# Out-projection weights of a Hymba-style block: ready-made high and low parts of the weight sums

## The chip, the cores and the metric

One core of one Trainium2 chip runs the whole kernel. The metric is the device time of one execution in microseconds (us); the median of three runs is quoted for the kernel before.

## The reference

One decoder layer on x of 2048 tokens x 1024 channels (D_MODEL), float32 throughout:

```python
h = rmsnorm(x, norm_pre_mix)
z = h @ w_in                    # columns: gMLP u, v; FoX q, k, v, gate; memory q
out_a = gmlp_spatial_gating(g_u, g_v, gmlp_w_s, gmlp_b_s, gmlp_v_norm)
out_b = forgetting_attention(f_q, f_k, f_v, log_sigmoid(f_gate + b_forget))
out_c = memory_cross_attention(m_q, rmsnorm(mem), w_mem_kv)
y = concatenate([out_a, out_b, out_c]) @ w_out
x = x + rmsnorm(y, norm_post_mix)
f = square(relu(rmsnorm(x, norm_pre_ffn) @ w_ff1)) @ w_ff2
x = x + rmsnorm(f, norm_post_ffn)
```

gMLP has 6 groups of 64 channels and works in chunks of 128 tokens, forgetting attention has 6 heads of 64 with a causal mask, memory attention 4 heads over 256 memory rows. w_out is 1024 x 1024, w_ff1 1024 x 4096.

## The kernel before

**Arithmetic.** A float32 factor is held as two parts of a rounded format: hi is the rounded value (ACT copies it), lo the rest (`src - hi`, on DVE unless told otherwise; `split`, L194 to 197). A product is three matmuls, hi·hi, hi·lo and lo·hi (`mm3`, L203 to 205). Large products use a seven-product scheme over 2 x 2 blocks: instead of eight block products there are seven, taken in the order 1, 7, 2, 6, 4, 5, 3, of sums of blocks. Products 1, 2 and 3 take a block of the weights as it is; 7, 5, 6 and 4 take a sum.

**Stages.** For each half s = 0, 1 of the tokens a rows stage (norm, transposes, value columns) is followed by a columns stage (`columns_stage`) with four jobs n = 0 to 3 that make the queries, keys and memory queries. Then come attention and gating in one stage, whose instructions on PE, DVE, ACT and POOL stand in an order that a planner (`plan`) works out from costs and due times written beside each `op`, the out-projection (`out_pair(j)`, a pair of token tiles at a time), and the feed-forward part.

**The weight sums of the out-projection.** w_out is read as 2 x 2 blocks of 512 x 512, in four slices kk = 0 to 3 of 128 rows. `out_sums(kk, sc)` runs behind job n = kk of the columns stage of s = 0. It loads both row slices into `wor{kk}` (1 MB, from a pool of two tiles that the jobs' own weights `wrc` share), makes four sums on DVE (L518 to 521; the tiles `wos` share four buffers with the jobs' weight sums `sc`) and stores each as float32 (L523) in the DRAM tensors `ws_d`.

**How the sums are used.** `out_weights` (L951) is part of the plan. For m = 1, 7, 2, 6 (EARLY) and each kk it loads a 128 x 512 slice (SP, L959), rounds it (ACT, L966, `wo0`) and makes the low part (DVE, L969, `wo1`), in the attention stage's last stretch. `late_weights` (L1275) does the same for m = 4, 5, 3 (LATE) through `fill` at the out-projection's start: loads of L264, splits of L195 and L197. As its float32 pieces need room, `low` tiles of one m serve as the raw tile of another.

**Around it.** The out-projection reads the context of the attention as `cr{j}` (SP, L1290; two tiles in turn), sums it on POOL (L1294 to 1297, `cs`), splits it (`cx`), multiplies and adds up `y`; y4's second half is a sum on POOL (`added(nc.gpsimd, ...)`, L1329). In the attention, `s` are scores (PE, L826 and 827), `k` and `q` the keys and queries loaded by SP (L189, L699), `cb` the forgetting bias rows (L802), `v` the values, `hr` the rows for the gating product (L986), `pt`, `ph`, `pl` the softmax's numbers with their high and low parts (DVE, L753, makes `pl`), `pv` the product with the values (PE, L767), `gl` a low part in the gating (POOL, L1167). SP issues DMA transfers in the order of its rows; a row that waits holds those behind it.

Of the kernel before, what the change touches and what calls it, by code (L numbers as in the profile page):

```python
# [16 lines left out]
P = 128  # L17
# [34 lines left out]
class Plan:  # L52
# [11 lines left out]
    def op(self, engine, time, fn, after, at, takes=(), frees=(), late=0.0):  # L64
        o = Op(engine, time, fn, after, at, takes, frees, late)
        self.ops.append(o)
        return o
# [62 lines left out]
def kernel(  # L130
# [35 lines left out]
    def dram(name, shape, dt=F32):  # L166
        return dp.tile(shape, dt, name=name, tag=name)
# [8 lines left out]
    x1_d = dram("x1_d", [NT, P, D], F32)  # L176
    bq_d = [dram(f"bq{s}", [4, P, 4, KT // 2, P]) for s in range(NSB)]
    b_d = [{m: dram(f"b{s}_{m}", [P, 4, KT // 2, P]) for m in range(1, 8)} for s in range(NSB)]
    ws_d = {m: dram(f"ws_{m}", [KT // 2, P, 512]) for m in (7, 5, 6, 4)}
    vm_d = dram("vm_d", [P, 2, NMH, 2 * HD])  # L180
    km_d = [dram(f"km{w}", [2, P, NM]) for w in range(2)]
    hid_d = [
# [326 lines left out]

    def out_sums(kk, sc):  # L510

        raw = rp.tile([P, 2, D], F32, name=f"wor{kk}", tag="raw")
        for half in range(2):
            r0 = (half * KH + kk) * P
            nc.sync.dma_start(raw[:, half], w_out[r0 : r0 + P, :])
        b11, b12, b21, b22 = [raw[:, a, b * 512 : (b + 1) * 512] for a in range(2) for b in range(2)]
        sm = {m: sc.tile([P, 512], F32, name=f"wos{kk}_{m}", tag="s") for m in (7, 5, 6, 4)}
        nc.vector.tensor_tensor(out=sm[7], in0=b22, in1=b12, op=ALU.subtract)  # L518
        nc.vector.tensor_tensor(out=sm[5], in0=b12, in1=b11, op=ALU.subtract)
        nc.vector.tensor_tensor(out=sm[6], in0=b22, in1=sm[5], op=ALU.subtract)  # L520
        nc.vector.tensor_tensor(out=sm[4], in0=b21, in1=sm[6], op=ALU.subtract)
        for m, t in sm.items():
            nc.sync.dma_start(ws_d[m][kk], t)  # L523


    def memory_keys(w1p, cp_):
# [60 lines left out]
    def columns_stage(s, h):  # L587
        with ExitStack() as st:
# [7 lines left out]
            for n, (ca, cb, *to) in enumerate(jobs):  # L596
                nm = f"c{s}_{n}"
                if n == 0:
                    raws = [xp.tile([P, D], F32, name=f"wr{i}{nm}", tag="x") for i in range(2)]
                    raws = [t.rearrange("p (k c) -> p k c", k=KH) for t in raws]  # L600
                else:
                    raw = rp.tile([P, KT, 2 * P], F32, name=f"wr{nm}", tag="raw")
                    raws = [raw[:, :KH], raw[:, KH:]]
                w = column_weights(
                    raws, sc, w1p, nm, (w_in[:, ca : ca + P], w_in[:, cb : cb + P]), True,
                    nc.gpsimd if n else nc.vector,
                )

                def emit(f, tn, c, own, nm=nm, to=to):
                    scale, dst, p = to[3 * f : 3 * f + 3]  # L610
                    hi = cp_.tile([P, 512], F32R, name=f"oh{f}{tn}_{nm}", tag="oh")
                    lo = cp_.tile([P, 512], F32R, name=f"ol{f}{tn}_{nm}", tag="ol")
                    split(hi, lo, c, scale=scale)
                    t0 = s * SB + tn * 512
                    store(dst[0][p][:, t0 : t0 + 512], hi)
                    store(dst[1][p][:, t0 : t0 + 512], lo)

                pend = columns(nm, w, h, kp, cp_, (ps_x, "x"), (ps_y, "y"), emit, pend)
                if s == 0:
                    out_sums(n, sc)  # L620
                elif n == 0:
                    forget_sums()
                elif n == 1:
                    memory_keys(w1p, cp_)
                elif n == 2:
                    gating_weights(row_weights("wua"), range(4))
# [11 lines left out]

    def out_block(m, kk):

        if m in ws_d:
            return ws_d[m][kk]
        r0, c0 = {1: (0, 0), 2: (KH, 0), 3: (KH, 512)}[m]
        return w_out[(r0 + kk) * P : (r0 + kk + 1) * P, c0 : c0 + 512]

    def flat(w, kk):
        return w[:, kk].rearrange("p k t -> p (k t)")
# [2 lines left out]
    with ExitStack() as st:  # L650
# [36 lines left out]
        def chain(name, new):  # L687

            new.after.append(order.get(name))
            order[name] = new  # L690
            return new
# [258 lines left out]

        def out_weights(near, after, at):  # L951

            for n in range(len(EARLY) * KH):
                m, kk = EARLY[n // KH], n % KH
                t = {}

                def wload(n=n, m=m, kk=kk, t=t):
# [14 lines left out]

                o = op("SP", 0.73, wload, [near], at, takes=["p", "wor"], late=3.0)
                o = chain("wh", op("ACT", 0.478, whigh, [o, after], at))
                op("DVE", 0.602, wlow, [o], at, frees=["p", "wor"])

        held = []
# [289 lines left out]
    with ExitStack() as st:  # L1267
# [5 lines left out]
        gpre = bcast_row(io, norm_pre_ffn[0], D, "gain_pre2")  # L1273

        def late_weights():  # L1275
            raws = dict(zip(LATE, [low[LATE[0]], low[LATE[2]], extra]))
            lows = dict(zip(LATE, [low[LATE[1]], low[LATE[0]], low[LATE[2]]]))
            wo.update(
                fill("wo", LATE, raws, lows, high, lambda m: [
                    (lambda t, k=k: flat(t, k), out_block(m, k), None, ()) for k in range(KH)  # L1280
                ])
            )
            low.update(lows)

        def out_pair(j):

# [369 lines left out]
```

## Time and profile before

| | before |
|---|---|
| median of 3 runs | 2270.11 us (2264.58, 2270.87, 2270.11) |
| the profiled execution's own time | 2261.8 us |
| its span in the profile | 2260.0 us |
| mean granted TensorE clock | 0.988 |
| PE busy | 2166.3 us (96%) |

The span runs from the first to the last instruction of the profiled execution. PE is the matmul engine, PEld its weight loads, DVE the vector engine, ACT the scalar engine, POOL GpSimd, SP the engine whose queue issues most DMA transfers (SPq in the rows). A busy share is an average over stages, so the windows of single stages say more than the totals.

### The profile page before, as it was taken

Reading aid. Unit: us, or ns where it says so; the run is one execution under the profiler, and the core shown is the slowest. Engines: PE = TensorE matmul, PEld = TensorE weight load, DVE = VectorE, ACT = ScalarE, POOL = GpSimd, SP = SyncE. Lnnn points to the kernel's source line nnn. Section 1 sums busy time; section 2 is a strip of 40 time slices with the busy share of each in tenths; the row PEclk is TensorE's granted clock in tenths of the full one; section 3 lists DMA queues with packets and bytes.
Section 4 is the critical chain, followed back from the end, with each engine's and each line's share of the span. In section 5 each row is a group of like instructions: output and inputs, shape, how many; then the busy total and the mean of one; then the engine's idle time right before and its main releaser. Section 6 shows DMA issues by size and latency. Waiting matters only on the chain.

```text
span 2260.0 us, 33156 instructions
## 1 busy us (share of the span) xinstructions
PE 2166.3 (96%) x10468; PEld 1820.0 (81%) x10468; DVE 1646.4 (73%) x3137; ACT 1354.3 (60%) x2929; POOL 1030.5 (46%) x1073
## 2 busy tenths in 40 slices
PE   7999989999999989998999999999999999999997
PEld 7787778888888867876888878888788888888885
DVE  8778667777867789895333366555579998999888
ACT  6455567878877766665555576666654443444333
POOL 5444432443535255544333335446465445534524
PEclk9999999999999999999999999999999999999999
DMA  7775685365363265786333365565132212221277
GB/s 248 261 252 174 226 224 132 88 169 137 95 157 95 79 216 202 246 307 205 112 109 110 112 205 195 192 231 199 56 130 86 91 48 95 92 94 57 94 253 296
DMA packets 236843, 359.98 MB, mean 159 GB/s; under 512 B 24806, under 2 KB 141420, under 8 KB 235644
## 3 DMA queue, kind: packets, MB, share of 16 engines
q1 hardware_dynamic: 224380, 316.92, 44.4%
q0 software_dynamic: 12288, 40.95, 4.9%
q8 instruction: 83, 1.36, 0.3%
q14 instruction: 92, 0.75, 0.1%
HBM read 232.88 MB, written 124.91 MB: 158 GB/s over the span
## 4 chain that ended last, share of the span: by engine, by line
PE 74%; DVE 8%; DMA 7%; issue 4%; ACT 4%; POOL 2%; SPq 1%; DVEq 0%; POOLq 0%; ACTq 0%
PE gx L205 5%; PE gx L204 5%; PE gx L203 5%; PE fxf L204 5%; PE fxf L203 5%; PE fxf L205 5%; PE pt L745 3%; PE gy L205 2%; PE gy L204 2%; PE gy L203 2%; PE fyf L203 2%; PE fyf L204 2%; PE fyf L205 2%; PE pv L767 2%; PE pv L766 2%
## 5 line engine op out<-in xcount | busy, mean ns | idle before, releaser
L205 PE MATMUL fxf<-h,w_f 128*128 128x512 f32 x512 | 201.1, 393 | 4.5 <-DVE w_f L197 4.5
L203 PE MATMUL gx<-w,hc 128*128 128x512 f32 x512 | 199.0, 391 | 5.9 <-DVE ya L1539 5.9
L204 PE MATMUL fxf<-h,w_f 128*128 128x512 f32 x512 | 200.6, 392 | 2.3 <-DVE h L197 2.3
L195 ACT ACTIVATE hc<-hs 128x256 fp32r<-128x256 f32 x224 | 93.6, 418 | 181.3 <-PE gx L205 105.7
L203 PE MATMUL fxf<-h,w_f 128*128 128x512 f32 x512 | 200.8, 392 | 1.0 <-ACT w_f L195 0.5
L204 PE MATMUL gx<-w,hc 128*128 128x512 f32 x512 | 199.7, 390 | 0.0
L205 PE MATMUL gx<-w,hc 128*128 128x512 f32 x512 | 195.9, 390 | 0.0
L197 DVE TENSOR_TENSOR w_f<-sf,w_f 128x512 fp32r<-128x512 f32 x128 | 95.4, 745 | 134.1 <-ACT w_f L195 132.3
L1539 DVE TENSOR_TENSOR ya<-gx,ya 128x512 f32<-128x512 f32 x232 | 156.5, 683 | 40.8 <-PE gx L205 40.6
L753 DVE TENSOR_TENSOR pl<-pt,ph 128x512 fp32r<-128x512 f32 x240 | 140.8, 605 | 45.3 <-ACT ph L749 43.6
L866 ACT ACTIVATE p<-p,nm 128x512 f32<-128x512 f32 (+2 forms) x240 | 156.9, 657 | 22.5 <-DVE nm L856 22.2
L749 ACT CAST ph<-pt 128x512 fp32r<-128x512 f32 x240 | 120.4, 523 | 59.5 <-PE pt L745 51.7
L197 DVE TENSOR_TENSOR w_f<-wrf,w_f 128x512 fp32r<-128x512 f32 x96 | 80.8, 841 | 88.4 <-ACT w_f L195 88.4
L195 ACT ACTIVATE w_f<-sf 128x512 fp32r<-128x512 f32 x128 | 80.8, 632 | 102.2 <-PE fxf L204 57.2
L837 DVE CUSTOM_DVE_ANT_0 p<-s,cb 128x512 f32<-128x512 f32 (+2 forms) x216 | 124.7, 593 | 16.8 <-PE pt L745 9.4
L197 DVE TENSOR_TENSOR hc<-hs,hc 128x256 fp32r<-128x256 f32 x224 | 128.1, 574 | 7.3 <-ACT hc L195 7.2
L195 ACT ACTIVATE hc<-hr 128x256 fp32r<-128x256 f32 x168 | 68.4, 417 | 103.2 <-PE gx L205 66.7
L745 PE MATMUL pt<-ident,p 128*128 128x128 f32 x816 | 124.0, 277 | 2.7 <-ACT p L866 2.7
L816 POOL TENSOR_TENSOR cm<-cb,cmask 128x128 f32<-128x128 f32 x96 | 44.8, 467 | 171.3 <-DVE mx L837 140.9
L1379 POOL TENSOR_TENSOR hs<-hr 128x256 f32<-128x256 f32 x56 | 51.7, 923 | 152.0 <-DMA hr<-hid 79.9
L745 PEld LDWEIGHTS pt<-ident,p 128*128 128x128 f32 x816 | 102.3, 143 | 22.6 <-ACT p L866 2.9
L203 PEld LDWEIGHTS gx<-w,hc 128*128 128x128 f32 x512 | 96.3, 188 | 27.4 <-DVE ya L1539 7.6
(389 smaller groups left out, 7105.8 us busy)
## 6 DMA issues: line engine op xcount, KB each, us to landing
wrf<-in_w_ff_dram SPq DMA_DIRECT2D x64, 512.0 KB, 4.8
hid<-c_f SPq DMA_DIRECT2D x128, 256.0 KB, 2.5
hr<-hid SPq DMA_DIRECT2D x56, 512.0 KB, 4.3
w2r<-in_w_ff_dram SPq DMA_DIRECT2D x16, 1024.0 KB, 6.7
b<-ty POOLq DMA_DIRECT2D x56, 256.0 KB, 3.7
hs<-lh SPq DMA_DIRECT2D x56, 256.0 KB, 2.7
hc<-hs SPq DMA_DIRECT2D x56, 256.0 KB, 5.2
xt<-in_x_dram SPq DMA_DIRECT2D x16, 512.0 KB, 4.4
```

Of the source, the lines that this page charges most:

```text
L195: a = nc.scalar.activation(hi, src, AF.Copy, scale=scale)
L197: return a, (eng or nc.vector).tensor_tensor(out=lo, in0=src, in1=f32(hi), op=ALU.subtract)
L203: nc.tensor.matmul(acc, lh, rh, start=first, stop=False, skip_group_check=more)
L204: nc.tensor.matmul(acc, lh, rl, start=False, stop=False, skip_group_check=more)
L205: nc.tensor.matmul(acc, ll, rh, start=False, stop=last, skip_group_check=more)
L745: nc.tensor.transpose(pt[:, a * P : (a + 1) * P], source(a, j), ident)
L749: nc.scalar.copy(hi[:, a0 * P :], tiles["pt", j][:, a0 * P :])
L753: nc.vector.tensor_tensor(out=lo[:, a0 * P :], in0=tiles["pt", j][:, a0 * P :], in1=f32(tiles["hi", j][:, a0 * P :]), op=ALU.subtract,)
L837: nc.vector.tensor_tensor_reduce(out=pr[:, cols], in0=t["s", a, c][:, cols], in1=sub, scale=1.0, scalar=-3.0e38, op0=ALU.subtract, op1=ALU ...
L866: nc.scalar.activation(pr, pr, AF.Exp, bias=t["nm", a], accum_out=t["rs"][:, a, c : c + 1])
L1379: eng.tensor_tensor(out=sm[7], in0=a11, in1=a21, op=ALU.subtract)
L1539: nc.vector.tensor_tensor(out=y, in0=a, in1=y, op=ALU.add)
```

## The change

`ws_d` holds two tensors for each m: the high and the low part of each slice. `out_sums` makes both behind the sums: ACT writes the high part into the quarter of the raw tile that no sum needs any more, and the low part replaces the sum, on POOL for m = 7 and 6, on DVE for 5 and 4. That makes eight stores of 256 KB per kk instead of four. The slice kk = 3 leaves the columns stage of s = 0 and comes behind job n = 3 of s = 1, right ahead of the attention. In `out_weights` m = 7 and 6 are now two loads of 1 MB each (`out_parts`), issued after the first rounding of m = 1; m = 1 and 2 are split as before. In `late_weights` m = 4 and 5 are loaded in the same way, m = 3 is split from a raw tile of its own, and no low tile serves as a raw tile any more.

```diff
-    ws_d = {m: dram(f"ws_{m}", [KT // 2, P, 512]) for m in (7, 5, 6, 4)}
+    ws_d = {m: [dram(f"ws{w}_{m}", [KT // 2, P, 512]) for w in range(2)] for m in (7, 5, 6, 4)}
...
-        for m, t in sm.items():
-            nc.sync.dma_start(ws_d[m][kk], t)
+        for (m, t), hi in zip(sm.items(), (b11, b12, b21, b22)):
+            nc.scalar.activation(hi.bitcast(F32R), t, AF.Copy)
+            (nc.gpsimd if m in (7, 6) else nc.vector).tensor_tensor(out=t.bitcast(F32R), in0=t, in1=hi, op=ALU.subtract)
+            nc.sync.dma_start(ws_d[m][0][kk], hi)
+            nc.sync.dma_start(ws_d[m][1][kk], t)
...
-                if s == 0:
-                    out_sums(n, sc)
+                if n == 3 or s == 0:
+                    if (s, n) != (0, 3):
+                        out_sums(n, sc)
...
-        if m in ws_d:
-            return ws_d[m][kk]
...
+    def out_parts(m):
+
+        for w in range(2):
+            load(wo[m][w].rearrange("p a k t -> p a (k t)"), ws_d[m][w].rearrange("a p c -> p a c"))
...
+            first = None
             for n in range(len(EARLY) * KH):
                 m, kk = EARLY[n // KH], n % KH
+                if m in ws_d:
+                    if kk == 0:
+                        op("SP", 0.12, lambda m=m: out_parts(m), [first], at, late=8.0)
+                    continue
...
                 o = chain("wh", op("ACT", 0.478, whigh, [o, after], at))
+                first = first or o
...
-            raws = dict(zip(LATE, [low[LATE[0]], low[LATE[2]], extra]))
-            lows = dict(zip(LATE, [low[LATE[1]], low[LATE[0]], low[LATE[2]]]))
-            wo.update(
-                fill("wo", LATE, raws, lows, high, lambda m: [
-                    (lambda t, k=k: flat(t, k), out_block(m, k), None, ()) for k in range(KH)
-                ])
-            )
-            low.update(lows)
+            for m in LATE:
+                if m in ws_d:
+                    wo[m] = [block_tile(at[m], f"wo{w}_{m}") for w, at in enumerate((high, low))]
+                    out_parts(m)
+                    continue
+                wo.update(
+                    fill("wo", (m,), {m: extra}, low, high, lambda m: [
+                        (lambda t, k=k: flat(t, k), out_block(m, k), None, ()) for k in range(KH)
+                    ])
+                )
```

The change also moves instructions. In the rows below, line numbers of the changed kernel are 8 to 16 higher than those of the same code before; a tile's last number is a counter.

SP at the passage from the columns of s = 1 to the attention, before (`b6` and `cb0_0` are the first loads of the attention, q and k the first head pair's queries and keys, each in a high and a low half):

```order
L676 DMA b6_3105<-in_gmlp_b_s_dram 6x128
L802 DMA cb0_0_3124<-c_d_84 128x512
L189 DMA v0_0_3126<-v_d_83 128x4x128
L802 DMA cb0_1_3133<-c_d_84 128x512
L189 DMA v0_1_3135<-v_d_83 128x4x128
L802 DMA cb0_2_3227<-c_d_84 128x512
L189 DMA q0_0_1_3113<-qhi_0_67 64x512
...
L189 DMA k0_0_3121<-khi_0_73 64x512
L699 DMA k0_0_3121<-klo_0_76 64x512
L986 DMA hr0_3112<-bq0_91 128x512 x2
L189 DMA k0_1_3130<-khi_0_73 64x512
L699 DMA k0_1_3130<-klo_0_76 64x512
```

and with the change:

```order
L526 DMA ws0_6_111<-wor3_3039 128x512
L526 DMA ws0_4_113<-wor3_3039 128x512
L684 DMA b6_3157<-in_gmlp_b_s_dram 6x128
L527 DMA ws1_6_112<-wos3_6_3044 128x512
L527 DMA ws1_4_114<-wos3_4_3045 128x512
L810 DMA cb0_0_3176<-c_d_84 128x512
L189 DMA q0_0_1_3165<-qhi_0_67 64x512
...
L189 DMA k0_0_3173<-khi_0_73 64x512
L707 DMA k0_0_3173<-klo_0_76 64x512
L189 DMA v0_0_3178<-v_d_83 128x4x128
L189 DMA k0_1_3182<-khi_0_73 64x512
L1000 DMA hr0_3164<-bq0_91 128x512 x2
L707 DMA k0_1_3182<-klo_0_76 64x512
```

Four of the eight stores of kk = 3 now come among the attention's first loads; the first values and the later bias rows go from ahead of q and k to behind them, and the hr0 loads from ahead of both halves of k0_1 to between them.

DVE at the attention's end, before (`wor` are the float32 slices of the early weights, `pl5_2_*` the low parts of the last head's last block):

```order
L753 TENSOR_TENSOR pl5_2_2_10553<-pt5_2_2_10526,ph5_2_2_10545 128x512
L753 TENSOR_TENSOR pl5_2_3_10557<-pt5_2_3_10540,ph5_2_3_10550 128x512
L969 TENSOR_TENSOR wo1_2_10272<-wor8_10493,wo0_2_10271 128x512
L753 TENSOR_TENSOR pl5_2_4_10584<-pt5_2_4_10563,ph5_2_4_10579 128x512
L753 TENSOR_TENSOR pl5_2_5_10592<-pt5_2_5_10574,ph5_2_5_10586 128x512
L969 TENSOR_TENSOR wo1_2_10272<-wor9_10537,wo0_2_10271 128x512
L969 TENSOR_TENSOR wo1_2_10272<-wor10_10548,wo0_2_10271 128x512
L753 TENSOR_TENSOR pl5_2_6_10615<-pt5_2_6_10594,ph5_2_6_10604 128x512
L969 TENSOR_TENSOR wo1_2_10272<-wor11_10555,wo0_2_10271 128x512
L753 TENSOR_TENSOR pl5_2_7_10626<-pt5_2_7_10607,ph5_2_7_10617 128x512
L969 TENSOR_TENSOR wo1_6_10274<-wor12_10572,wo0_6_10273 128x512
```

and with the change:

```order
L982 TENSOR_TENSOR wo1_2_10324<-wor9_10508,wo0_2_10323 128x512
L982 TENSOR_TENSOR wo1_2_10324<-wor10_10526,wo0_2_10323 128x512
L982 TENSOR_TENSOR wo1_2_10324<-wor11_10535,wo0_2_10323 128x512
L761 TENSOR_TENSOR pl5_2_2_10602<-pt5_2_2_10580,ph5_2_2_10590 128x512
L761 TENSOR_TENSOR pl5_2_3_10604<-pt5_2_3_10593,ph5_2_3_10599 128x512
L761 TENSOR_TENSOR pl5_2_4_10628<-pt5_2_4_10609,ph5_2_4_10623 128x512
L761 TENSOR_TENSOR pl5_2_5_10635<-pt5_2_5_10618,ph5_2_5_10630 128x512
L761 TENSOR_TENSOR pl5_2_6_10652<-pt5_2_6_10637,ph5_2_6_10645 128x512
L761 TENSOR_TENSOR pl5_2_7_10659<-pt5_2_7_10647,ph5_2_7_10654 128x512
```

The splits of m = 2 move ahead of these low parts, to the places where those of m = 7 stood, and none stands among or behind them.

POOL at the out-projection's start, before (`cs0` and `cs1` are the context sums of the first and the second pair, `y4` the first pair's last sum):

```order
L1297 TENSOR_TENSOR cs0_3_10808<-cr0_10802,cs0_6_10807 128x512
L1294 TENSOR_TENSOR cs1_7_11070<-cr1_11067 128x512
L1295 TENSOR_TENSOR cs1_5_11071<-cr1_11067 128x512
L1296 TENSOR_TENSOR cs1_6_11072<-cs1_5_11071,cr1_11067 128x512
L1297 TENSOR_TENSOR cs1_3_11073<-cr1_11067,cs1_6_11072 128x512
L1329 TENSOR_TENSOR y4_10819<-ko4_0_10977,ko7_0_10903 128x512
```

and with the change:

```order
L1313 TENSOR_TENSOR cs0_3_10832<-cr0_10826,cs0_6_10831 128x512
L1345 TENSOR_TENSOR y4_10843<-ko4_0_10979,ko7_0_10905 128x512
L1310 TENSOR_TENSOR cs1_7_11072<-cr1_11069 128x512
L1311 TENSOR_TENSOR cs1_5_11073<-cr1_11069 128x512
L1312 TENSOR_TENSOR cs1_6_11074<-cs1_5_11073,cr1_11069 128x512
```

The sum of y4 moves from behind the second pair's sums to ahead of them. On SP the loads of cr1 move from ahead of those of cr2 to behind them.

## Rows read from the trace of the kernel before

**Rows 1.** The page's part 1: busy us, share of the span, instructions.
```profile
PE 2166.3 (96%) x10468; PEld 1820.0 (81%) x10468; DVE 1646.4 (73%) x3137; ACT 1354.3 (60%) x2929; POOL 1030.5 (46%) x1073
```

**Rows 2.** Windows: stretch, us, busy PE, PEld, DVE, ACT, POOL, PEclk, DMA share, GB/s.
```profile
64.00:137.00 73.00, 72.87 (x314) 58.79 (x313) 53.86 (x65) 32.05 (x58) 35.05 (x41) 1.00 0.74 252
194.00:285.00 91.00, 87.91 (x434) 72.64 (x432) 65.78 (x109) 47.06 (x84) 39.41 (x51) 1.00 0.65 202
285.00:308.00 23.00, 15.73 (x70) 12.64 (x69) 10.21 (x40) 12.78 (x29) 12.94 (x22) 0.85 1.05 311
776.00:806.00 30.00, 21.18 (x85) 15.40 (x83) 26.98 (x69) 25.83 (x55) 14.84 (x21) 0.75 0.33 95
806.00:821.00 15.00, 12.07 (x67) 9.18 (x67) 14.17 (x24) 10.12 (x20) 9.10 (x10) 0.94 0.40 134
821.00:836.00 15.00, 15.00 (x72) 12.04 (x70) 13.16 (x16) 10.68 (x20) 7.18 (x5) 1.00 0.77 240
836.00:860.00 24.00, 21.73 (x92) 16.86 (x92) 18.34 (x25) 14.65 (x31) 13.89 (x10) 1.00 0.70 260
```

**Rows 3.** Groups of the tiles wo and cr: ns min/median/max, first and last start.
```profile
L966 ACT CAST wo<-wor x16: 609/622/631, 777.4 to 817.5; 128x512 fp32r<-128x512 f32 x16
L969 DVE TENSOR_TENSOR wo<-wor,wo x16: 673/685/1532, 778.1 to 819.2; 128x512 fp32r<-128x512 f32 x16
...
L1294 POOL TENSOR_TENSOR cs<-cr x8: 1282/1296/1798, 819.9 to 953.0; 128x512 f32<-128x512 f32 x8
```

**Rows 4.** SP's timeline at attention's start (start us, us); then a DMA issue.
```profile
277.33 0.35 SPq L802 DMA_DIRECT2D cb<-c_d  x1
...
284.02 0.44 SPq L189 DMA_DIRECT2D k<-khi  x1
...
287.54 1.37 SPq L986 DMA_DIRECT2D hr<-bq  x2
289.04 0.45 SPq L189 DMA_DIRECT2D k<-khi  x1
...
cb<-c_d SPq DMA_DIRECT2D x3, 256.0 KB, 5.1
```

**Rows 5.** PE's timeline there; in brackets the idle time before and its releaser.
```profile
291.61 0.48 PE L826 MATMUL s<-k,q 128*128 128x512 f32 x1 [2.60 <-DMA k<-klo]
295.41 0.55 PE L826 MATMUL s<-k,q 128*128 128x256 f32 x1 [3.10 <-DMA k<-klo]
```

**Rows 6.** The windows view, four us ahead of the attention.
```profile
280.00:284.00 4.00, 4.00 (x19) 3.25 (x18) 1.66 (x5) 0.95 (x2) 0.00 (x0) 1.00 1.04 301
```

**Rows 7.** PE's timeline at the attention's end and in the out-projection.
```profile
813.38 0.50 PE L767 MATMUL pv<-pl,v 128*128 128x512 f32 x1 [1.38 <-DVE pl L753]
...
848.64 0.50 PE L203 MATMUL ox<-wo,cx 128*128 128x512 f32 x1 [1.12 <-ACT cx L195]
...
850.37 0.50 PE L205 MATMUL ox<-wo,cx 128*128 128x512 f32 x1 [1.00 <-DVE cx L197]
```

**Rows 8.** Groups of the tile gl: whole run, then 800 to 820.
```profile
L1167 POOL TENSOR_TENSOR gl<-z,gh x16: 994/1014/1452, 457.6 to 812.1; 128x384 fp32r<-128x384 f32 x16
...
L1167 POOL TENSOR_TENSOR gl<-z,gh x4: 1016/1446/1452, 808.3 to 812.1; 128x384 fp32r<-128x384 f32 x4
```

**Rows 9.** POOL's timeline in the out-projection.
```profile
837.48 1.30 POOL L1294 TENSOR_TENSOR cs<-cr 128x512 f32<-128x512 f32 x1 [9.22 <-DVE cx L197]
...
843.51 1.73 POOL L1329 TENSOR_TENSOR y<-ko,ko 128x512 f32<-128x512 f32 x1
```

**Rows 10.** SP's timeline at cr2, and the DMA issues of cr, 800 to 862.
```profile
831.57 1.22 SPq L1290 DMA_DIRECT2D cr<-ctx  x2
...
cr<-ctx SPq DMA_DIRECT2D x7, 512.0 KB, 5.8
```

## The prediction

> **What bounds the kernel now.** I read the busy totals first: PE is busy 2166.3 of the span, with DVE next at 1646.4 [rows 1]. So off-PE work counts only where PE waits for it. The windows by stage show where that is [rows 2]. In the columns of the first half (64 to 137 us) PE is busy 72.87 of 73.00, and DVE, ACT and POOL have 19.1, 40.9 and 37.9 us to spare. At attention's start (285 to 308) PE has 7.3 us idle and the DMA engines are full. At its end, 776 to 806, PE is busy 21.18 of 30 at a granted clock of 0.75, a mean of its two levels (2.4 and 1.2 GHz); from 806 to 821 it is idle 2.93 us, and from 836 to 860, in the out-projection, 2.27. The change adds work to the first of these places, shifts transfers at the second and removes work from the others. The PE program itself keeps its matmuls and almost their order, so the sum is one of waits.
>
> **Prices.** One 128x512 operation takes 0.622 us as an ACT hi, 0.685 as a DVE lo, and 1.296 as a POOL sum [rows 3]; no POOL subtract with a rounded output of that shape is in the trace, so I take 1.3 for it. For one over 128x384 POOL has 1.014 and, at its worst, 1.452 [rows 8], which per element is 1.35 to 1.94, so 1.3 to 1.9 bounds it.
>
> **A, the sums in the columns.** For kk=0 to 2 there are 4 hi, 2 POOL lo and 2 DVE lo each: ACT 12 x 0.62 = 7.5, POOL 6 x 1.3 = 7.8 (11.4 at 1.9), DVE 6 x 0.685 = 4.1, less DVE's four sums of kk=3 at about the same 0.685, 2.7. All fits the slack above. DMA gains 12 stores of 256 KB (3.1 MB) and loses kk=3's 1 MB load and four stores (2.1 MB): 1.0 MB more beside 73 x 252 = 18.4 MB, at a share of 0.74 [rows 2]. SP now has two of the stores between the two halves of the next job's weights; two stores are 0.52 MB, 2.1 us at 252 GB/s. I take 0, since a job lasts 18 us and its weights come a job ahead; the bounds are 0 and +2.1. If that cover went, the full 2.1 would fall on PE.
>
> **B, kk=3 at attention's start.** Its eight stores come in SP's last rows ahead of attention, and those that wait for ACT, POOL or DVE hold what follows on that queue. Before, cb0_0 was issued at 277.33 [rows 4]. Now the last five stores come as late as that; at half of hr0's 1.37 for two issues [rows 4], five are 3.4 us, so I put it at about 281. But four loads of 256 KB (v0_0, cb0_1, v0_1, cb0_2) leave the place ahead of q and k, so the first key should still go at its 284.02, and the first scores still start near 291.61 [rows 5]. What is late is the second key: its low half comes behind the two hr0 loads, whose issue takes 1.37, and cb0_1 behind that: 289.04 + 0.45 + 1.37 + 0.6 = 291.5, and 5.1 to landing [rows 4] gives 296.6, where the scores that wait for k now start at 295.41 [rows 5]. That is +1.2. The DMA engines are already full just before, share 1.04 at 280 to 284 [rows 6]; were all five stores (1.31 MB) to go ahead of the keys at 311 GB/s it would be +4.2, and if the POOL, ACT and DVE rows finish early, 0. Range 0 to +4.2, I take +1.2, as the row at 295.41 is the nearest.
>
> **C, the early weights (m=7 and 6).** Eight ACT hi (5.0 us) and eight DVE lo go; four 1 MB loads replace eight of 256 KB, 2.1 MB more in a stretch at 95 GB/s, so they land long before 824. The order puts m=2's splits where m=7's stood, so up to about 806 DVE's row is as full as before (26.98 of 30), and what falls away is behind: 806 to 821, DVE 14.17 of 15 busy. There lo's last up to 1.532 [rows 3] beside POOL's gl, whose last four take 1.446 instead of 1.014 [rows 8]. PE's wait at 813.38 (1.38, released by DVE's pl) is of this kind [rows 7]. I take three gl that no longer wait, 3 x 0.43 = 1.3, and half of that PE wait, 0.7: -2.0. The bounds are 0 (what PE waits for there may be the chain of softmax and gating alone) and -2.9, all its idle time.
>
> The Trainium skill, "SBUF — State Buffer", section "Who interferes with whom", says that a DVE instruction with two SBUF inputs and a GpSimd instruction that reads SBUF share a port pair, and that the second blocks for the whole of the first. The gl row shows 0.43 lost, not a whole 0.685, so this trace agrees in kind and not in size. By that rule the four gl would give 4 x 0.685 = 2.7 here, the sum would be -3.2 and the time 2266.9. It also speaks against the change: six to eight POOL subtracts now stand beside DVE splits in the columns, where their 7.8 to 11.4 us would still be under DVE's spare 19.1.
>
> **D, the late weights (m=5 and 4).** Eight ACT hi and eight DVE lo go from behind attention; only m=3's four pairs remain. Two PE waits stood behind them, 1.12 at 848.64 and 1.00 at 850.37, both for cx, ACT's and DVE's splits of the second pair [rows 7]: -2.1. The new order puts something in their place. cr1's two loads go behind cr2's, which wait for cr0's last reader (831.57 before); with 5.8 to landing [rows 10] that is some 838 to 839 for cr1. POOL has y4's sum (1.73) ahead of cs1_7, where before it came at 843.51 behind all four cs1 [rows 9]; so cs1_7 moves from 837.48 to about 842. And ACT's hi of the second pair's m=7 now stands behind the copy of its m=1, so the product of m=7 waits for one hi and one lo, 1.3, less the copy's overlap: about 1.1. So -2.1 + 1.1 = -1.0. The bounds are -2.3, all idle time of 836 to 860, and +1.7, if y4's 1.73 falls whole on PE. The bytes of m=5 and 4 double (2.1 MB more in 821 to 836, at 240 GB/s and a share of 0.77); m=4 is the fifth product, and PE was without a gap there [rows 2], so this is 0 within B's and D's bounds.
>
> **Sum.** 0 + 1.2 - 2.0 - 1.0 = -1.8 us on the profiled execution (2261.8 us, its span 2260.0). That gives 2260.0; the median of the three runs shown is 8.3 us above it, so on that footing 2270.1 - 1.8 = 2268.3. The bounds sum to -5.2 and +8.0. A measurement of this kernel can tell about 0.3% (6.8 us) from no change: its three runs lie 6.3 us apart.
>
> **Rivals.**
> 1. Faster. DVE (91% busy from 776 to 821) is what makes PE pause there: with eight operations fewer on it and eight on ACT, all idle time of C and D goes (5.2), and the stretch at 0.75 gets shorter by 30 x 0.25 x 0.7 = 5.3, 0.7 being PE's busy share. -10.5: 2259.6. For it: DVE is fuller there than anywhere else. Against it: up to 806 the order leaves as many splits as before. 0.20.
> 2. Slower. kk=3 is made too late: its last stores issue behind 284.02, the keys wait on SP behind them, and the 1.05 MB load and 2.1 MB of stores fall whole into the stretch with full DMA: 3.1 MB at 311 GB/s = 10.1, less the 3.0 of C and D: 2277.2. It decides if the stores' last row issues after 284. Against it: POOL, ACT and DVE have a quarter or more free from 194 to 285 [rows 2]. 0.15.
> 3. No gain. At the end PE waits for POOL's sums or for cr1 instead, C is the softmax chain; only B is left, +1.2: 2271.3. 0.20.
>
> **Numbers.** The forecast (a small gain, 2268.3) has 0.45. The range 2260 to 2276 takes in the bounds of the sum up to +5.9 and most of rivals 1 and 3; it leaves out half of rival 1 and most of rival 2, about 0.2. Rival 1 is the one beyond -0.3%, 0.2; rival 2 beyond +0.3%, 0.15; the rest, 0.65, is within it.
>
> **What would show it.** A: no new PE gap in the columns. B: the first scores within 0.5 us of 291.61 and the second key's about 1 us later than 295.41. C: 806 to 821 shorter by 2, gl near 1.0, lo's gone. D: the waits of 848.64 and 850.37 gone and one of about 1 us for the second pair's m=7. I am wrong if columns of the first half last over 2 us longer, if keys are issued after 285, or if 776 to 806 shrinks with its clock above 0.8.

## The result: slower by half a per cent

The change takes 2279.51 us (median of 6 runs, 2275.2 to 2285.19) against 2269.3 us for the kernel before (6 runs, 2264.58 to 2271.37). The ratio is 1.0050, with a 95% interval of 1.0038 to 1.0062: about 10 us slower, where I had forecast 2 us faster, and outside my range.

The profiled execution of the change took 2285.19 us (span 2283.5), the slowest of its six, and that of before (2261.8) lies below all of its timed runs. A second profile of the kernel before (2267.97 us) differs from the first by 3 us in a stage and 7 in all, so I read a single difference below some 3 us as scatter, unless rows show its cause or other profiles repeat it.

Windows of the change (columns as in [rows 2]) for the same work as those of before:

```profile
64.00:82.00 18.00, 17.37 (x75) 13.82 (x74) 13.58 (x18) 8.46 (x15) 8.13 (x7) 1.00 0.79 265
82.00:100.00 18.00, 18.00 (x79) 14.57 (x79) 14.10 (x17) 8.69 (x16) 8.35 (x11) 1.00 0.79 269
100.00:118.00 18.00, 13.62 (x48) 10.18 (x47) 11.18 (x9) 6.74 (x13) 11.86 (x12) 0.81 0.77 252
...
300.00:310.00 10.00, 3.04 (x9) 2.16 (x10) 1.98 (x7) 1.29 (x3) 2.32 (x5) 0.65 1.06 347
...
792.00:822.00 30.00, 20.09 (x82) 14.45 (x81) 26.34 (x68) 25.27 (x54) 15.64 (x21) 0.77 0.68 220
822.00:836.00 14.00, 13.61 (x80) 10.82 (x78) 8.96 (x18) 6.97 (x14) 8.04 (x10) 0.89 0.20 73
836.00:851.00 15.00, 14.62 (x63) 11.80 (x64) 8.73 (x10) 6.36 (x12) 7.16 (x5) 1.00 1.03 378
851.00:875.00 24.00, 21.56 (x95) 16.20 (x94) 17.30 (x22) 14.64 (x30) 12.74 (x10) 1.00 0.65 248
```

Two new holes stand in PE's work: 4.4 us from 100 to 118, with the granted clock at 0.81 (in [rows 2] PE had 0.13 us idle in all of 64 to 137), and 7 of 10 us from 300 to 310. At the end the forecast shows: the stretch that answers to 806 to 821 has PE busy 13.61 of 14 us, and DVE fell from 14.17 of 15 to 8.96 of 14.

To compare many kernels I use **the shift**: how much later PE starts the same matmul than in the first profile of before (the median of nine matmuls that follow the named moment of before, from the two PE timelines). Us, worked out from the traces:

```
moment of before             139   191   285   335   776   862
before, second profile       1.2   1.4   4.5   3.2   5.8   6.9
the change                   6.9   7.5   9.8  16.4  16.0  14.9
the change, second profile   6.7   7.4   9.5  15.2  15.2  13.2
e4 end alone                 0.9   1.2   2.7   1.2   2.8   1.9
e5 slice kk=3 moved alone   -0.2  -0.5   1.2   0.5   3.4   5.5
e6 low parts on DVE          1.7   2.4   5.1  12.5  14.8  14.3
e13 bias row first           5.6   5.3   8.4  11.7  14.5  13.5
e14 e13, low parts on DVE    2.1   3.9   6.8  10.7  15.1  13.7
e15 best version             2.2   2.3   7.3   4.3   2.6   0.8
```

So the change loses some 5.5 us in the first half's columns (139), 6 us at the attention's start (285 to 335), and gains 1 to 2 at the end (776 to 862); both its profiles agree. Together that is some 10 us, the timed difference. The spans of the profiles differ by more (2283.5 and 2277.7 against 2260.0 and 2266.2): part of that is a jump behind 862 that comes and goes ("The profiles again", below).

**The first hole.** DVE, ACT, POOL and PE of the change around it (start us, us):

```profile
102.16 1.11 DVE L197 TENSOR_TENSOR w_c<-sc,w_c 128x512 fp32r<-128x512 f32 x1 [3.62 <-ACT w_c L195]
...
104.89 5.43 DVE L197 TENSOR_TENSOR w_c<-wrc,w_c 128x512 fp32r<-128x512 f32 x1
...
101.50 0.63 ACT L195 ACTIVATE w_c<-sc 128x512 fp32r<-128x512 f32 x1 [4.13 <-POOL sc L289]
...
100.18 1.29 POOL L289 TENSOR_TENSOR sc<-wrc 128x512 f32<-128x512 f32 x1 [4.24 <-DMA ws<-wos]
101.43 1.29 POOL L525 TENSOR_TENSOR wos<-wos,wor 128x512 fp32r<-128x512 f32 x1
102.68 1.73 POOL L290 TENSOR_TENSOR sc<-wrc 128x512 f32<-128x512 f32 x1
...
104.91 0.54 POOL L192 DMA_DIRECT2D khi<-oh_c  x1
105.46 1.29 POOL L291 TENSOR_TENSOR sc<-sc,wrc 128x512 f32<-128x512 f32 x1
106.69 0.56 POOL L192 DMA_DIRECT2D klo<-ol_c  x1
107.26 1.28 POOL L322 TENSOR_TENSOR c_c<-k_c,k_c 128x512 f32<-128x512 f32 x1
108.49 1.27 POOL L292 TENSOR_TENSOR sc<-wrc,sc 128x512 f32<-128x512 f32 x1
109.70 0.56 POOL L192 DMA_DIRECT2D khi<-oh_c  x1
...
110.37 0.79 PE L205 MATMUL fzc<-hc,w_c 128*128 128x512 f32 x1 [3.98 <-DVE w_c L197]
```

POOL waits 4.24 us for a store of the low part to land, since the sums of the next job share their four buffers with `wos`. ACT's next split waits 4.13 for the first of these sums, and DVE 3.62 for ACT. Then POOL's late work comes in one piece, and a DVE split that takes 0.685 elsewhere takes 5.43 beside it. PE waits for that split.

**The second hole**, at the attention's start:

```profile
292.08 0.44 SPq L810 DMA_DIRECT2D cb<-c_d  x1
...
295.76 0.55 SPq L189 DMA_DIRECT2D k<-khi  x1
...
300.78 0.32 SPq L810 DMA_DIRECT2D cb<-c_d  x1
...
301.83 0.47 PE L834 MATMUL s<-k,q 128*128 128x512 f32 x1 [3.07 <-DMA k<-klo]
307.44 0.58 PE L834 MATMUL s<-k,q 128*128 128x256 f32 x1 [4.91 <-DMA k<-klo]
...
308.90 0.45 POOL L824 TENSOR_TENSOR cm<-cb,cmask 128x128 f32<-128x128 f32 x1 [6.85 <-DMA cb<-c_d]
```

Less the shift of 9.8 there, the first key is issued at 286.0 (284.02 before), and the second bias row at 291.0 (before, the second cb load was issued 2.4 us behind the first, ahead of q). It lands 8.0 us later, and POOL's masked row (`cm`), which the softmax of the first block needs, waits 6.85 us for it; in the kernel before it ran at 284.97.

### The profile page after: what moved, and what is told of

It is laid out like the page before. It is cut to its first block, busy times and chain, and to the rows that moved or that the text cites. A ratio compares the mean times of both kernels' runs of the same rounds, so it can differ in the third digit from the quotient of the medians.

```text
span 2283.5 us, 33177 instructions
## 1 busy us (share of the span) xinstructions
PE 2178.3 (95%) x10468; PEld 1830.4 (80%) x10468; DVE 1640.8 (72%) x3129; ACT 1354.6 (59%) x2929; POOL 1041.6 (46%) x1081
```

## The experiments

Ratios are to the kernel before, from timed runs on the same chip, with 95% intervals. Each diff is against the change unless it says otherwise.

**e2: slice kk=3 back in the first half.**

```diff
-                if n == 3 or s == 0:
-                    if (s, n) != (0, 3):
-                        out_sums(n, sc)
+                if s == 0:
+                    out_sums(n, sc)
```

> The whole change, but slice kk=3 stays behind job 3 of the first half's columns. Theory 1 (two places cost: the first half's columns, where the 100 to 118 us stretch has a PE stall of 4 us and a slower clock, 6.9 us of shift in all, and the attention's start, about 5 us of shift between 291 and 330): the second cost goes, so the ratio to the kernel before falls from 1.005 to about 1.003, and the first scores of the second key come no later than the columns' own shift. Theory 2 (the attention's start is only noise of the profiled run): the ratio stays at 1.005. A third outcome is that a fourth set of splits in the first half adds a stall of its own before 140 us, another 2 to 5 us.

Ratio 1.0066 (1.0048 to 1.0085), no better than the change. The shift stays flat from 285 to 335 (27.0, 26.9), so the loss at the attention's start is real and belongs to this slice; but by 191 the shift is 22.7. It comes nearest to the third outcome, but the new loss is some 14 us where I had allowed 5, and it falls behind 140 (shift at 139: 8.7), not ahead of it.

**e3: both stores take the high part** (the low part is made and never leaves the core).

```diff
-            nc.sync.dma_start(ws_d[m][1][kk], t)
+            nc.sync.dma_start(ws_d[m][1][kk], hi)
```

> The whole change, but both stores of a sum take the high part, so the low part is computed and never leaves the core (the output lacks the low parts of four weight sums; bytes, stores and the work of ACT, DVE and POOL stay). The buffer of a sum is free once its low part is made, not once a store has landed. Theory 1 (the next job's weight sums wait for the low part's store to land, since they share four buffers): the 4 us PE stall near 110 us and its slow clock go, shift at 140 us falls from 6.9 to below 2, ratio about 1.002. Theory 2 (the six POOL subtracts themselves hold DVE up through the shared reads): the stall stays, DVE splits of 3 to 5 us beside POOL remain, ratio 1.005.

Ratio 1.0032 (1.0019 to 1.0046); the shift at 139 is 7.1. The stall near 110 is gone, but another one of the same size stands at 122.05, where PE waits 4.38 us for ACT's split of the next job's weights: SP had issued them behind four stores, and they landed late. The buffers are only one of the ways in which the slice delays its neighbours; neither theory had this one. Here too a DVE split takes 4.53, at 127.59 beside three POOL operations, and PE does not wait for it.

**e4: the end alone** (the columns as in the kernel before; high and low tiles both loaded from the float32 sums).

```diff
...
-            load(wo[m][w].rearrange("p a k t -> p a (k t)"), ws_d[m][w].rearrange("a p c -> p a c"))
+            load(wo[m][w].rearrange("p a k t -> p a (k t)"), ws_d[m].rearrange("a p c -> p a c"))
...
```

> The columns stages as before (four float32 stores a slice, kk=3 in its old place), and only the end of the change: m=7, 6, 5, 4 are loaded into the high and the low tiles, both from the float32 sums (the output is then off by these weights' low parts; loads, bytes and the missing splits are those of the change). Theory 1 (the end gives what the trace of the change shows there, 1.8 us up to the attention's end and little behind it): ratio 0.999, within 0.997 to 1.000. Theory 2 (the end itself is slower, through the doubled bytes or the wait for the second pair's m=7): ratio above 1.000, and PE idle in the out-projection's first 40 us above the 2.3 us of before.

Ratio 0.9981 (0.9968 to 0.9994): the end alone gains 1.4 to 7 us of 2270. Its windows:

```profile
809.00:823.00 14.00, 13.40 (x79) 10.79 (x77) 8.81 (x18) 7.00 (x14) 7.90 (x10) 0.88 0.27 80
823.00:838.00 15.00, 14.63 (x63) 11.82 (x64) 8.72 (x10) 6.35 (x12) 7.12 (x5) 1.00 1.05 392
```

PE has 0.6 us idle in the first, where before it had 2.93 in 15 [rows 2].

**e5: slice kk=3 moved alone** (the kernel before, with the change's condition on `(s, n)` and float32 sums).

> The kernel before with only one part of the change: slice kk=3 (load, four sums, four float32 stores) behind job 3 of the second half, no splits there and the old end. Theory 1 (what costs at the attention's start is that this slice's rows and stores stand in SP's queue ahead of the first keys): a shift of 2 to 6 us between 285 and 335, ratio 1.001 to 1.003. Theory 2 (it takes the splits: eight stores and their waits for ACT and POOL): shift below 1.5 us, ratio 1.000.

Ratio 0.9992 (0.9979 to 1.0005); the shift from 285 to 335 goes from 1.2 to 0.5. Moving the slice costs nothing; the eight stores and the splits do.

**e6: all low parts on DVE.**

```diff
-            (nc.gpsimd if m in (7, 6) else nc.vector).tensor_tensor(out=t.bitcast(F32R), in0=t, in1=hi, op=ALU.subtract)
+            nc.vector.tensor_tensor(out=t.bitcast(F32R), in0=t, in1=hi, op=ALU.subtract)
```

> The whole change, but all four low parts of a slice are made on DVE, none on POOL. Theory 1 (buffers that wait for stores): the PE stall near 110 us stays at 2 to 4 us, the ratio at 1.004 to 1.005. Theory 2 (POOL's subtracts, its queue in order and the shared reads): the stall goes, shift at 140 us below 2 us, ratio about 1.002.

Ratio 1.0022 (1.0007 to 1.0036): more than half of the loss is gone, and it went in the columns (shift at 139: 1.7; in this one profile most of it is lost again by 776). The same window, then the group of the jobs' DVE splits from 60 to 145 (ns min/median/max), here and in the change:

```profile
100.00:118.00 18.00, 18.00 (x79) 14.48 (x78) 14.38 (x19) 10.17 (x18) 8.85 (x11) 1.00 0.89 291
...
L197 DVE TENSOR_TENSOR w_c<-wrc,w_c x9: 677/683/1784, 77.7 to 129.5; 128x512 fp32r<-128x512 f32 x9
```
```profile
L197 DVE TENSOR_TENSOR w_c<-wrc,w_c x9: 680/690/5427, 75.7 to 134.5; 128x512 fp32r<-128x512 f32 x9
```

The second theory held: with the stores on SP, POOL's subtracts are what stalls the first half. The first theory has a share in it, since the wait runs over a store. Rows ahead of the first hole show how, the change first, then e6:

```profile
90.28 1.61 POOL L525 TENSOR_TENSOR wos<-wos,wor 128x512 fp32r<-128x512 f32 x1 [2.29 <-ACT wor L524]
...
93.98 1.82 SPq L527 DMA_DIRECT2D ws<-wos  x2
```
```profile
90.32 0.48 SPq L527 DMA_DIRECT2D ws<-wos  x1
...
96.56 1.58 POOL L289 TENSOR_TENSOR sc<-wrc 128x512 f32<-128x512 f32 x1 [2.07 <-DVE ol_c L198]
```

POOL makes the low part late, its store goes behind two weight loads on SP, 3.7 us later than in e6, and the next job's first sum, which waits for this store, starts at 100.18 instead of 96.56.

The loss at the attention's start stays (285 to 335: 7.4).

**e7 and e8: low parts on DVE, slice kk=3 elsewhere** (e7 behind job 3 of the first half, as in e2; e8 behind job 0 of the second).

> The change with all low parts on DVE and slice kk=3 behind job 3 of the first half. Theory 1 (POOL's subtracts made the first half stall; the 20 us that the slice cost there with them came from POOL's queue too): the first half shifts by less than 4 us, the attention's start by none, ratio 0.998 to 1.000. Theory 2 (a fourth slice with splits is too much for the first half whatever engine makes the low parts: the rows of the second half wait for DVE or SP): shift of 10 us or more between 118 and 191, ratio 1.003 or more.

> The change with all low parts on DVE and slice kk=3 behind job 0 of the second half, 70 us ahead of the attention. If the two causes named (POOL's low parts in the first half, the slice right ahead of the keys) are all that cost, what is left is the gain at the end: ratio 0.998, 0.997 to 0.999, and no shift between 285 and 335. If job 0's stores and splits make the second half's weights late, a shift of 2 to 6 us between 191 and 233 takes the gain: ratio 0.999 to 1.002.

Ratios 1.0037 (1.0023 to 1.0051) and 1.0047 (1.0029 to 1.0065). Neither loses at the attention's start, and both lose elsewhere, as the second outcome of each had it: e7 11.5 us between 139 and 191, e8 11 between 191 and 285, more than the 2 to 6 expected. SP's queue shows a part of it. In e7 the row for the second half's gain comes behind the slice's stores, at 144.12 instead of 132.56, and PE waits 3.82 for the rows; in e8 the next job's weights come at 214.43 instead of 192.07, and PE waits 1.49 for their split at 219.54. Longer waits of PE in e8 (3.22 at 196.91 for a DVE split, 2.79 at 243.46 for ACT's copy) are not explained by that row. The profiles of before, e7 and e8:

```profile
132.56 0.33 SPq L413 DMA_DIRECT2D gain_pre<-in_norm_pre_mix_dram  x1
...
192.07 3.34 SPq L286 DMA_DIRECT2D wrc<-in_w_in_dram  x4
```
```profile
144.12 0.33 SPq L413 DMA_DIRECT2D gain_pre<-in_norm_pre_mix_dram  x1
...
149.54 1.97 PE L431 MATMUL pt<-ident,h 128*128 128x128 f32 x8 [3.82 <-DVE h L399]
```
```profile
211.83 0.90 SPq L527 DMA_DIRECT2D ws<-wos  x2
214.43 2.20 SPq L286 DMA_DIRECT2D wrc<-in_w_in_dram  x4
```

**e9, e10, e11: the stores on ACT's queue** (e9 with low parts on DVE; e10 with nothing else; e11 as e9, slice kk=3 back in the first half).

```diff
-            nc.sync.dma_start(ws_d[m][0][kk], hi)
-            nc.sync.dma_start(ws_d[m][1][kk], t)
+            nc.scalar.dma_start(ws_d[m][0][kk], hi)
+            nc.scalar.dma_start(ws_d[m][1][kk], t)
```

> The change with two edits: all low parts on DVE, and the eight stores of a slice issued from ACT's queue instead of SP's. Slice kk=3 stays right ahead of the attention. Theory 1 (at the attention's start the keys are late because SP's queue is held by stores that wait for their splits): the first key is issued as early as without the slice, the shift between 285 and 335 falls from 7 us to below 2, ratio 0.998 (0.997 to 1.000), the gain of the end alone. Theory 2 (the work of ACT and DVE and the 2.1 MB are what costs there): the shift stays at 4 us or more, ratio 1.001 or more. ACT issues eight stores a slice itself, so a PE wait for ACT in the first half is a third way to lose.

> The change with the stores on ACT's queue alone; POOL still makes two low parts a slice. Theory 1 (two causes that add: POOL's low parts in the first half, SP's queue at the attention's start): the first half still shifts by about 5 us with a DVE split of 3 us or more beside POOL, the attention's start by less than 2: ratio 1.001 (1.000 to 1.003). Theory 2 (SP's queue was behind both, since it issues the next job's weights too): no stall in the first half, ratio 0.998 to 0.999.

> As e9, but slice kk=3 behind job 3 of the first half, where it cost 12 us with stores on SP (the loads for the second half's rows stood behind them). Theory 1 (SP's queue): the shift between 139 and 191 falls below 3 us, ratio 0.997 to 0.999. Theory 2 (the work itself is too much there): a shift of 8 us or more stays, ratio 1.002 or more.

Ratios 1.0027 (1.0014 to 1.0041), 1.0012 (0.9999 to 1.0024) and 1.0030 (1.0018 to 1.0042). SP's queue is not all. The first key goes no earlier for it: at the q loads SP now waits for a store of the slice to land (5.0 us in e9, 5.7 in e10), and the key goes at 286.0 and 288.7, less the shift. In e9 the second key's scores do start early, but the shift from 285 to 335 is still 5.7 (9.7 to 15.4). POOL again waits for the bias row, 2.77; the longer wait is DVE's 5.27 for the next masked row, which stands on POOL behind low parts of the rows hr (`ht`), and these wait for ACT, which waits for the loads of hr:

```profile
302.18 0.58 PE L834 MATMUL s<-k,q 128*128 128x256 f32 x1 [0.48 <-DMA k<-klo]
...
304.27 0.45 POOL L824 TENSOR_TENSOR cm<-cb,cmask 128x128 f32<-128x128 f32 x1 [2.77 <-DMA cb<-c_d]
...
306.03 0.62 ACT L1089 CAST ht<-hr 128x512 fp32r<-128x512 f32 x1 [6.62 <-DMA hr<-bq]
...
309.62 1.26 POOL L1092 TENSOR_TENSOR ht<-hr,ht 128x512 fp32r<-128x512 f32 x1 [1.62 <-ACT ht L1089]
310.85 0.45 POOL L824 TENSOR_TENSOR cm<-cb,cmask 128x128 f32<-128x128 f32 x1
...
311.34 0.29 DVE L845 CUSTOM_DVE_ANT_0 p<-s,cm 128x128 f32<-128x128 f32 x1 [5.27 <-POOL cm L824]
```

Its columns lose too (7.3 at 139; a wait of 3.15 for DVE's split). In e10 the shifts are 4.2 at 139 and 3.2 from 285 to 335: both places better, with POOL's subtracts still there. So POOL's share in the first half depends on when its rows fall; e9 with none on POOL was no better than e10. In e11 the fourth slice costs 7.5 between 139 and 191 whatever the queue: its second theory, nearly to the number. SP's load of the gain waits there until 147.16 for a store on ACT's queue to land.

All profiles together, by how much the shift grows from 64 to 139:

| stores of the slices | low parts | profiles | us |
|---|---|---|---|
| float32, on SP | none | e0, e4, e5 | -1.5 to 1.4 |
| on SP | two on POOL | the change twice, e2, e3, e13 | 4.1 to 7.1 |
| on SP | all on DVE | e6, e7, e8, e12, e14, e15 | 0.1 to 1.5 |
| on ACT | either | e9, e10, e11 | 4.4 to 5.9 |

**e13 and e14: the bias row ahead of its key** (e14 with low parts on DVE as well).

```diff
-                    kk[c] = load_pair(f"k{h}_{c}", "k", khl[0][p], khl[1][p], half, ks)
                     cc[c] = kv.tile([P, QB], F32, name=f"cb{h}_{c}", tag="cb", bufs=4)
                     nc.sync.dma_start(cc[c], c_d[h, ks].partition_broadcast(P))
+                    kk[c] = load_pair(f"k{h}_{c}", "k", khl[0][p], khl[1][p], half, ks)
```

> The change with one move: each bias row (cb) is loaded ahead of its key instead of behind it, all else as in the change. Theory 1 (what costs at the attention's start is that cb0_1 comes some 8 us later, and POOL's masked row, DVE's maxima and ACT's exponentials wait for it): POOL's wait for cb falls from 6.9 us to below 3, the shift between 285 and 335 from 6.6 to 3 or less, ratio 1.003. Theory 2 (the keys' own lateness and the full DMA engines cost it): the shift stays at 5 us or more, ratio 1.005.

> e13 with all low parts on DVE. If POOL's low parts in the first half (5 us) and the late bias row (3 to 4 us) are separate causes that add, ratio 1.000 (0.999 to 1.001), against 1.0022 with the low parts on DVE alone. If the bias row does not matter, it stays at 1.002.

Ratios 1.0038 (1.0024 to 1.0053) and 1.0007 (0.9994 to 1.0020). POOL's wait falls from 6.85 to 1.28 and 1.10; e13, then e14:

```profile
302.73 0.45 POOL L824 TENSOR_TENSOR cm<-cb,cmask 128x128 f32<-128x128 f32 x1 [1.28 <-DMA cb<-c_d]
```
```profile
300.23 0.45 POOL L824 TENSOR_TENSOR cm<-cb,cmask 128x128 f32<-128x128 f32 x1 [1.10 <-DMA cb<-c_d]
```

The shift from 285 to 335 falls to 3.3 and 3.9, about half of what it was without the edit (6.6 and 7.4). The timed intervals overlap with those of the change and of e6, so the size rests on the two traces; what is left goes with the keys' own lateness (waits of 3.81 and 5.59 for klo in e13). It does not last: from 285 to 776 e13 loses 6.1 and e14 8.3, against 6.2 and 9.7 without the edit. So the bias row is shown to hold the attention's first blocks, and not that half of the loss is its price; what takes the rest of the attention is open.

**e12 and e15: slice kk=3 stays float32 and is split at the end** (slices 0 to 2 as in e6; e12 with kk=3 behind job 3 of the first half, e15 behind job 3 of the second).

```diff
+            if kk == 3:
+                nc.sync.dma_start(ws_d[m][0][kk], t)
+                continue
...
-            load(wo[m][w].rearrange("p a k t -> p a (k t)"), ws_d[m][w].rearrange("a p c -> p a c"))
+            load(wo[m][w].rearrange("p a k t -> p a (k t)")[:, :3], ws_d[m][w][:3].rearrange("a p c -> p a c"))
...
+                    hi, lo = [flat(t, 3) for t in wo[m]]
+                    nc.sync.dma_start(f32(lo), out_block(m, 3))
+                    split(hi, lo, f32(lo))
```

> Slices kk=0 to 2 as in the change with their low parts on DVE; slice kk=3 as in the kernel before (float32 sums, stored behind job 3 of the first half), loaded and split at the end, one split for each of m=7, 6, 5, 4 where the kernel before has four. Theory 1 (the gain lies at the end and three quarters of it stay; DVE makes the low parts in the first half for nothing): no shift above 2 us before 335, the end 1 to 3 us shorter, ratio 0.999 (0.997 to 1.000). Theory 2 (the splits in the first half cost about 2 us even on DVE, and eight stores a slice delay the rows): ratio 1.001.

> e12 with slice kk=3 (float32 sums, four stores, split at the end) ahead of the attention, where it cost nothing as float32, instead of behind job 3 of the first half, where the loads of the second half's rows stood behind the stores. Theory 1 (the named costs are all): no shift above 2 us up to 335 us, ratio 0.9985 (0.997 to 0.9995), faster than the kernel before. Theory 2 (the three slices split on DVE in the first half cost the gain too): ratio 1.000 or more.

e12: 1.0015 (1.0005 to 1.0024), with 10 us lost between 139 and 191 at the second half's rows, although its fourth slice has only four stores. e15: **0.9982 (0.9973 to 0.9992)**, median 2266.84 us against 2271.11 beside it: faster than the kernel before and than the change, the ratio of its first theory. With four stores instead of eight there, the attention's first loads stand in SP's queue as they did before; the shift changes by -3.0 from 285 to 335 and by -1.8 from 776 to 862. (Its 7.3 at 285, more than the 2 us of that theory, is no lasting loss of this kernel that I can name; the second profile of before has 4.5 there.) Its windows at the attention's start and the end:

```profile
292.00:315.00 23.00, 16.93 (x74) 13.56 (x73) 10.70 (x44) 12.97 (x30) 13.25 (x23) 0.85 1.04 315
...
809.00:823.00 14.00, 13.68 (x78) 10.59 (x76) 10.27 (x19) 7.19 (x15) 8.34 (x10) 0.89 0.25 86
```

**The profiles again.**

> The kernel before, unchanged, for a second profile of it. If the shift of 4 us that the change and two of its variants show at 1037 to 1050 us, in the feed-forward part's start, is scatter from one execution to the next, this profile shows it too against the first one; if it belongs to the change, this profile has it not.

> The change itself, for a second profile. The DVE split of 5.4 us near 105 us and the PE stall of 4 us behind it repeat, as do POOL's wait for the bias row at the attention's start and the 5 to 7 us lost there; the jump of 4 us at 1037 to 1050 us may be missing, since the kernel before and some variants show none.

The second profile of before has no jump at 1037 to 1050 us; both of the change have it (3.9 and 5.5 us). e4, e6, e13 and e14 show 3 to 4 us there too, e3 5.1 and e15 2.1, but e2, e7, e8 and e10 at most 0.6, though their end is the same, and e4 and e15 are faster in spite of it. What makes it stays open. In the second profile of the change the longest split of that group is 3.86 us and the stall comes in two parts, 1.65 near 81 and 1.07 near 110, with the granted clock at 1.00 from 100 to 118 and nearly the same shift at 139: the loss repeats, its exact place does not. POOL's wait for the bias row repeats, at 6.08.

## Why the prediction was wrong

**A, the first half's columns: forecast 0 (0 to +2.1), measured about 5.5.** The sentence that failed is "All fits the slack above". I had added up POOL's 7.8 us against 37.9 us of idle time. But the idle sum says nothing of when POOL's rows can run: a subtract waits for its hi (2.29 at 90.28), the next job's sum for the subtract's store (4.24 at 100.18), and ACT and DVE for that sum. e6 takes POOL's subtracts away and the shift at 139 falls from 6.9 to 1.7, about that of the second profile of before (1.2); the table of all profiles says the same wherever the stores are on SP.

The Trainium skill, "SBUF — State Buffer", section "Who interferes with whom", says that a GpSimd instruction that reads SBUF and a DVE instruction with two SBUF inputs exclude each other, the second blocked for the whole of the first. I had called the trace weaker than that rule, from the gl row. The split of 5.43 us is stronger: it stood through three POOL operations (1.29, 1.28 and 1.27) and three DMA issues of POOL. Its row starts 0.57 us ahead of the first of the three operations, where by that rule POOL would have waited, so the rule does not account for all of it. The rule spoke against the change, and I let the sum over the stage outweigh it. Yet a split so held is not enough to cost PE: e6, e7 and e8 have one of 3.50 to 4.41 near 103 (of `ol_c`), beside POOL's sums alone, and PE does not wait for it. In the change the held split is one for PE's next product, late already from the waits above.

**B, the attention's start: forecast +1.2 (0 to +4.2), measured 5.7 to 6.6.** "The first key should still go at its 284.02" failed: it went at 286.0. The issue time of the second bias row was right (291.0 against 291.5), its price was not: I took 5.1 to landing where it took 8.0, and let only the scores wait, while the wait runs over POOL's cm to DVE's maxima (6.11 at 309.38). The first scores start at 292.0 less the shift, within the 0.5 us forecast, those of the second key at 297.6, 2.2 later than before where I had 1.2. e5 and e15 (no loss with four float32 stores) show that the eight stores with their splits cost it; e9 (second key early, loss still 5.7) and e13 and e14 (row early, loss up to 335 about halved) show that neither the keys nor the bias row is all of it. How the loss divides is open.

**C, 776 to 821: forecast -2.0, measured -0.7 and -1.1** in the two profiles. The mechanism was right: gl fell to 1.006 from the 1.446 of [rows 8], and the wait of 1.38 of [rows 7] is gone. The size was not: PE's idle time there fell from 2.93 of 15 us to 0.39 of 14, but the granted clock of the stretch is 0.89 against 0.94 (0.92 against 0.99 in the second profiles), so part of what the waits gave back went into slower matmuls; how much is not measured.

```profile
L1181 POOL TENSOR_TENSOR gl<-z,gh x4: 1002/1006/1009, 824.9 to 827.8; 128x384 fp32r<-128x384 f32 x4
```

**D, 821 to 862: forecast -1.0, measured -0.4 and -0.9.** The wait for the second pair's m=7 came as forecast, and y4's sum ahead of cs1. Of the two waits of [rows 7] the first is gone; the second is 0.41 at 865.79, and 1.20 in the second profile of the change, so it did not go for certain:

```profile
858.11 0.50 PE L203 MATMUL oy<-wo,cx 128*128 128x512 f32 x1 [1.20 <-ACT cx L195]
859.87 0.50 PE L205 MATMUL oy<-wo,cx 128*128 128x512 f32 x1 [0.51 <-DVE cx L197]
...
865.79 0.50 PE L205 MATMUL ox<-wo,cx 128*128 128x512 f32 x1 [0.41 <-DVE cx L197]
...
854.11 1.32 POOL L1345 TENSOR_TENSOR y<-ko,ko 128x512 f32<-128x512 f32 x1 [10.87 <-ACT ko L1334]
855.39 1.29 POOL L1310 TENSOR_TENSOR cs<-cr 128x512 f32<-128x512 f32 x1
```

The measured values of C and D are within the scatter of one profile, but rows show the cause, and the timed runs of the end alone (-1.4 to -7 us) hold the forecast of both together, -3.0.

**The rivals.** The nearest was the second (2277.2), but its mechanism holds only in part. Its point of decision, stores issued after 284, was not reached: the last one is issued by 292.08 less 9.8, 282.3. Nor is the loss the bytes: e10 moves as many and loses half as much there (3.2 against 6.6). Two signs that I had named for being wrong came, though: keys after 285, and columns over 2 us longer. I had priced POOL's queue in the columns nowhere.

## What to carry to other kernels

Work that fits the idle sum of an in-order engine or queue still costs, if it waits there for something and a neighbour's work stands behind it: before pricing an addition at nothing, ask what is queued behind each of its waits, on the engine and on the queue that issues its stores. A precomputation that doubles its stores wants a place where no load of the next stage is due; here three slices had one, and for the fourth the old form was cheaper (e15). Another queue is no sure cure: a later load that takes over the slice's buffers waits for its stores to land whichever queue they are on (5.0 us in e9).

## What I had not expected of the hardware

A DVE split with both inputs in SBUF took 5.43 us instead of 0.685 while POOL ran three operations of some 1.28 us and issued three transfers beside it; it is 5.44 in e2, and 3.86 is the longest of its group in the second profile. POOL's low parts are not needed for it: in e8, where POOL makes none, another split took 4.41 beside three sums of POOL. In the kernel before the longest of the first half's columns is 2.45.

```profile
103.29 4.41 DVE L197 TENSOR_TENSOR ol_c<-c_c,oh_c 128x512 fp32r<-128x512 f32 x1
```
